# GpSimd out of the weight splits of the expert stage, layer-norm factors spread by TensorE, and a ninth gather buffer

## The chip, the cores and the metric

One core of a Trainium2 chip runs the whole program; the other cores idle. The metric is the device time of one execution in microseconds (us). The engines are TensorE (PE; its weight loads are listed as PEld), VectorE (DVE), ScalarE (ACT), GpSimd (POOL) and SyncE (SP). SyncE issues the transfers of weights and outputs, GpSimd issues the gathers, and 16 DMA engines carry out both kinds.

## The reference, cut to what matters

Two blocks follow each other on 256 tokens of width 1024, in float32. The first (a Hyena mixer and a grouped-query attention) is not touched. The second has two layers, each a mixer (a gated linear recurrence, a state-space part and windowed attention) and a product-key expert layer:

```python
def second_block(x, ...):
    h = layer_norm(x, emb_ln_g, emb_ln_b)
    for l in range(DEPTH):                       # 2
        proj = h @ w_in[l]
        ...                                      # three mixers -> mix
        h = layer_norm(DN_ALPHA * h + mix, ln1_g[l], ln1_b[l])
        ffn = peer_ffn(h, peer_wq[l], peer_keys[l], peer_u[l], peer_v[l])
        h = layer_norm(DN_ALPHA * h + ffn, ln2_g[l], ln2_b[l])
    return h

def peer_ffn(x, wq, keys, u, v):                 # per chunk of 128 tokens
    ...                                          # 8 heads x 16 experts: idx, gate
    ue = u[idx]; ve = v[idx]
    act = gelu(einsum('td,thkd->thk', xc, ue))
    return einsum('thk,thkd->td', gate * act, ve)
```

Each token picks 128 of 16384 experts (8 heads, 16 each), and each expert is one row of `u` and one of `v`, 1024 numbers each. `layer_norm` is `(x - mean) * rsqrt(var + eps) * g + b`, with `g` and `b` of 1024 numbers; there are five such pairs.

## The kernel before, in words

The second block works on four units: layer 0 and tokens 0 to 127, layer 0 and tokens 128 to 255, then the same for layer 1. Here a unit's mixer is called work 0 to 3. Work 0 runs by itself. After that the experts of unit n run together with work n + 1.

**Experts** (`experts`). For each unit 128 gathers run (512 in all). One gather fetches for each of the 128 tokens one expert's row of `u` and `v`, 8 KB per partition, 1 MB in all, into a buffer `uv`; it is an indirect DMA that GpSimd issues (line 1258). VectorE forms the dot product with the token (line 1267, "the dot"). ScalarE applies the gelu for two gathers at a time (line 1271), multiplies by the gate (line 1278) and makes a diagonal matrix `dg` (line 1281). TensorE adds `dg @ v` to two accumulating banks `psG`, two matmuls of 128x512 (line 120, "the add"). The add frees the buffer. Eight buffers exist (`UV_BUFS`), the gathers are issued four ahead of the dots (`UV_BUFS - 4`), and the add comes three gathers after the dot.

**Mixer work** (`work`, a `Flow` of generators). After each gather's instructions the loop takes some steps of the next unit's flow, so many that it ends shortly before the unit's 128 gathers do (`per`, `owed`). Its matrices (60 loads of up to 512 KB, 120 pieces) come through four raw buffers on SyncE's queue. ScalarE rounds each piece to a high part `wh` (line 77); the low part `wl` is the difference of both (line 78, "the split"). `k.share` says who makes it: with 2 every second piece's split goes to GpSimd, with 4 every fourth, else to VectorE. Work 0 has 2, works 1 to 3 have 4. TensorE then needs three matmuls a piece.

**Layer norms.** `stats` forms mean and variance on VectorE, the power on GpSimd (`rsqrt`, line 124), and loads `g` and `b`, spread over all 128 partitions by the DMA, into four tiles `lng` of 256 KB (line 810). `scaled` applies them in two steps for each half of the row (lines 830 and 831). There are ten norms: two ahead of work 0, one in each work, one at the end of each unit's experts. The tiles `lng` also hold the recurrence's gate weights `rg_w` (line 1019).

**Order.** The program is written as these loops; a scheduler then orders each engine's instructions by modelled times, and moves DMAs forward to where it models their buffers free. Each engine runs its list in order: an instruction that waits holds up all behind it on its engine. This holds for DMA issues on SyncE and GpSimd as well.

PSUM has in this stage two banks each for `G` (the adds), `M` (the main stream: projections, output, the turns), `C` and `D`.

Of the kernel before, what the change touches and what calls it, by code (L numbers as in the profile page):

```python
# [20 lines left out]
P = 128  # L21
# [619 lines left out]
def peer_route(k, pool, kb, qT, t, h0, nh, idx, gate):  # L641
# [10 lines left out]
    for h in range(nh):  # L652
        ps = k.bank("D")
        k.mm(ps[:, :SEQ], qT[:, h0 + h, t * P:(t + 1) * P], kb)
        sc = T([P, 2, P], "psc", bufs=2)
        nc.scalar.copy(sc.rearrange("p a b -> p (a b)"), ps[:, :SEQ])
        for i in range(2):
            top16(k, pool, sc[:, i, :], ts_[:, h, i, :], tu[:, h, i, :], P)
            yield
# [39 lines left out]
def top16(k, pool, vals, top, idx, n):  # L699
    nc = k.nc  # L700
    rest = pool.tile([P, P], F32, tag="trs", name=k.uid("trs"), bufs=2)[:, :n]
    nc.vector.max(top[:, 0:8], vals)
    nc.vector.max_index(idx[:, 0:8], top[:, 0:8], vals)
    nc.vector.match_replace(rest, top[:, 0:8], vals, -3.0e38)
    nc.vector.max(top[:, 8:16], rest)
    nc.vector.max_index(idx[:, 8:16], top[:, 8:16], rest)
# [31 lines left out]
UV_BUFS = 8  # L738
# [3 lines left out]
class Second:  # L742


    def __init__(self, k, io, pool, h):
        self.k, self.io, self.pool, self.h = k, io, pool, h
        self.lay, self.kb, self.qT = {}, {}, {}
        self.idx = {}
        self.po = {}
        self.rs = {}  # L750

# [51 lines left out]
    def stats(self, t, i, src):  # L803

        k, nc = self.k, self.k.nc
        gb = []
        for j in range(2):
            for dh in range(2):
                w = self.T([P, 512], "lng", bufs=4)
                nc.sync.dma_start(w, self.io["ln_gb"][i, j, dh * 512:(dh + 1) * 512].partition_broadcast(P))  # L810
                gb.append(w)
# [10 lines left out]
        self.rs[t] = gb, mv, rs  # L822

    def scaled(self, t):
        nc = self.k.nc
        gb, mv, rs = self.rs.pop(t)
        r = self.h[t]
        for dh in range(2):
            cs = slice(dh * 512, (dh + 1) * 512)
            nc.vector.scalar_tensor_tensor(r[:, cs], r[:, cs], mv[:, 0:1], gb[dh], ALU.subtract, ALU.mult)  # L830
            nc.vector.scalar_tensor_tensor(r[:, cs], r[:, cs], rs, gb[2 + dh], ALU.mult, ALU.add)  # L831
# [174 lines left out]
    def left(self, l, t):  # L1006
# [10 lines left out]
        for i in range(2):  # L1017
            wbd.append(T([P, 512], "lng", bufs=4).rearrange("p (a c) -> p a c", a=4))
# [227 lines left out]
    def experts(self):  # L1246
# [51 lines left out]
        k.share = 4  # L1298
# [157 lines left out]
def layouts(x, c, ctx, c_ctx, norm_g, ada_w, ada_b, hy_w_in, hy_conv_w, hy_conv_b, hy_fw1, hy_fb1,  # L1456
# [98 lines left out]
    io["ln_gb"] = np.stack(gb).reshape(5, 2, D)  # L1555
# [34 lines left out]
```

## Time and profile before

| | |
|---|---|
| time, median of 3 runs | 2750.16 us (2749.62 to 2754.34) |
| profiled execution | 2752.02 us, its span 2750.3 us |
| mean granted TensorE clock | 0.958 of 2.4 GHz |
| busy: TensorE, VectorE, ScalarE, GpSimd | 2364.6, 2075.2, 1294.2, 1055.5 us |
| moved by DMA | 778.11 MB; gathers (queue 0) 536.90 MB |
| first gather issued | 1094.0 us |
| last dot | 2732.8 us |

The first block and work 0 take the time up to 1094 us; the expert stage takes the rest. The page's chain of waits holds hardly more than the last norm, so the stage is read from stretches of time, from the waits and from the order of time. In a row of stretches each engine's busy time is followed by its count of instructions; PEclk is the granted clock, and the DMA share is the mean busy share of the 16 DMA engines.

### The profile page before, as it was taken

To read this page: it belongs to the slowest core of one execution; us is meant where nothing else is said; L and a number is where in the kernel's file an instruction comes from. 1 tells how busy PE (TensorE), PEld (TensorE's weight loads), DVE (VectorE), ACT (ScalarE), POOL (GpSimd) and SP (SyncE) were. 2 spreads that over 40 slices of the span, in tenths; PEclk is the share of its full clock that TensorE was granted. 3 is DMA by queue.
4 is the path that set the end of the run, shared out by engine and by line. 5 is a ranking of instruction groups with operands and counts; after the bars stand their busy time and mean duration, and the time that the engine had idled before them with its cause. 6 is when DMAs were issued, how large, how long until landed. Compare 5 with 4: busy or idle time off the path is not lost. (4 is left out here: it accounts for less than half of the span.)

```text
span 2750.3 us, 30013 instructions
## 1 busy us (share of the span) xinstructions
PE 2364.6 (86%) x8930; PEld 1463.6 (53%) x8930; DVE 2075.2 (75%) x4579; ACT 1294.2 (47%) x2960; POOL 1055.5 (38%) x844
## 2 busy tenths in 40 slices
PE   8999999999998786788978888987788998777776
PEld 4788888857888454445533344544344544322222
DVE  6788887766887876799758589867689966964444
ACT  4444444434554664467534366734366753322222
POOL 0322223221210443544445455544444454343332
PEclk9999999999999797899999999999999999899999
DMA  6333332224333554999899999999999999899997
GB/s 245 123 106 112 111 108 90 79 90 149 118 104 116 189 178 156 413 393 358 340 398 392 413 401 373 399 386 383 389 405 381 360 372 368 343 404 421 421 422 306
DMA packets 149162, 778.11 MB, mean 283 GB/s; under 512 B 18663, under 2 KB 19464, under 8 KB 83464
## 3 DMA queue, kind: packets, MB, share of 16 engines
q0 software_dynamic: 73728, 536.90, 48.2%
q1 hardware_dynamic: 75272, 239.29, 24.4%
q8 instruction: 72, 1.18, 0.2%
q14 instruction: 90, 0.74, 0.1%
HBM read 775.08 MB, written 1.05 MB: 282 GB/s over the span
## 5 line engine op out<-in xcount | busy, mean ns | idle before, releaser
L120 PE MATMUL psG<-uv,dg 128*128 128x512 f32 x2048 | 1009.5, 630 | 235.4 <-ACT dg L1281 235.0
L1267 DVE CUSTOM_DVE_ANT_0 uv<-uv,h 128x1024 f32<-128x1024 f32 x512 | 648.1, 1270 | 308.5 <-DMA uv<-in_peer_uv_dram,idx 303.9
L1258 POOL DMA_INDIRECT uv<-in_peer_uv_dram,idx x512 | 602.9, 1177 | 455.6 <-PE psG L120 266.9
L120 PEld LDWEIGHTS psG<-uv,dg 128*128 128x128 f32 x2048 | 387.9, 199 | 706.7 <-ACT dg L1281 349.8
L77 ACT ACTIVATE wh<-w 128x512 fp32r<-128x512 f32 (+3 forms) x644 | 454.0, 721 | 483.8 <-PE psA L116 178.7
L78 DVE TENSOR_TENSOR wl<-w,wh 128x512 fp32r<-128x512 f32 (+3 forms) x494 | 441.9, 909 | 126.5 <-ACT wh L77 123.3
L78 POOL TENSOR_TENSOR wl<-w,wh 128x512 fp32r<-128x512 f32 (+1 forms) x150 | 233.0, 1554 | 541.5 <-issue 362.9
L1271 ACT ACTIVATE cf<-act 128x2 f32<-128x2 f32 x256 | 51.7, 202 | 545.2 <-DVE act L1267 544.6
L117 PE MATMUL psA<-hT1h,wl 128*128 128x512 f32 (+1 forms) x640 | 235.7, 369 | 2.4 <-DVE wl L78 2.4
L115 PE MATMUL psA<-hT1h,wh 128*128 128x512 f32 (+1 forms) x640 | 236.9, 371 | 0.0
L116 PE MATMUL psA<-hT1l,wh 128*128 128x512 f32 (+1 forms) x640 | 235.6, 368 | 0.0
L116 PE MATMUL psM<-wl,hTh 128*128 128x512 f32 (+1 forms) x352 | 180.5, 513 | 42.2 <-DVE wl L78 37.0
L115 PE MATMUL psM<-wh,hTh 128*128 128x512 f32 (+1 forms) x352 | 169.6, 484 | 22.9 <-DVE idx L689 12.8
L1281 ACT ACTIVATE dg<-ident,cf 128x128 f32<-128x128 f32 x512 | 174.9, 386 | 1.0 <-PE psG L120 1.0
L117 PE MATMUL psM<-wh,hTl 128*128 128x512 f32 (+1 forms) x352 | 142.6, 405 | 0.0
L115 PEld LDWEIGHTS psA<-hT1h,wh 128*128 128x128 f32 x640 | 120.6, 188 | 23.4 <-issue 0.9
L117 PEld LDWEIGHTS psA<-hT1h,wl 128*128 128x128 f32 x640 | 120.5, 188 | 23.1 <-DVE wl L78 2.8
L116 PEld LDWEIGHTS psA<-hT1l,wh 128*128 128x128 f32 x640 | 120.6, 188 | 19.9
L116 PEld LDWEIGHTS psM<-wl,hTh 128*128 128x128 f32 x352 | 71.3, 203 | 106.7 <-DVE wl L78 60.1
L1278 ACT ACTIVATE cf<-cf,gate 128x1 f32<-128x1 f32 x512 | 122.3, 286 | 6.6
L369 POOL TENSOR_TENSOR hm<-hx,hx 128x512 f32<-128x512 f32 x16 | 30.5, 1905 | 187.5 <-ACT hx L359 187.5
L115 PEld LDWEIGHTS psM<-wh,hTh 128*128 128x128 f32 x352 | 70.8, 202 | 57.1 <-issue 23.3
(417 smaller groups left out, 3813.9 us busy)
## 6 DMA issues: line engine op xcount, KB each, us to landing
w<-in_w_in_r_dram SPq DMA_DIRECT2D x128, 512.0 KB, 7.9
w<-in_hy_w_in_dram SPq DMA_DIRECT2D x64, 512.0 KB, 3.5
w<-in_w_out_dram SPq DMA_DIRECT2D x64, 512.0 KB, 6.0
w<-in_ada_w_dram SPq DMA_DIRECT2D x32, 512.0 KB, 3.5
w<-in_peer_wq_dram SPq DMA_DIRECT2D x32, 512.0 KB, 7.8
lng<-in_ln_gb_dram SPq DMA_DIRECT2D x40, 256.0 KB, 5.6
aw<-in_ada_w_dram SPq DMA_DIRECT2D x16, 512.0 KB, 8.6
w<-in_hy_w_out_dram SPq DMA_DIRECT2D x16, 512.0 KB, 3.5
```

The costliest lines, as they stand in the source:

```text
L77: nc.scalar.activation(dst.hi, src, AF.Copy)
L78: (eng or nc.vector).tensor_tensor(dst.lo, src, dst.hi.bitcast(F32), ALU.subtract)
L115: mm(out, a.hi, b.hi, start=start, stop=False)
L116: mm(out, a.hi, b.lo, start=False, stop=False)
L117: mm(out, a.lo, b.hi, start=False, stop=stop)
L120: self.nc.tensor.matmul(out, a, b, start=start, stop=stop)
L369: nc.gpsimd.tensor_tensor(m[:, ci, :], got[0], got[3], ALU.mult)
L1258: nc.gpsimd.indirect_dma_start(out=uv.rearrange("p a b -> p (a b)"), out_offset=None, in_=self.io[f"peer_uv{n // 2}"], in_offset=bass.Indi ...
L1267: nc.vector.tensor_tensor_reduce(u, u, self.h[i // P % 2], 1.0, 0.0, ALU.mult, ALU.add, acts[i // 2][:, i % 2:i % 2 + 1])
L1271: nc.scalar.activation(cfs[b], acts.pop(b), AF.Gelu)
L1278: nc.scalar.activation(cf[:, j:j + 1], cf[:, j:j + 1], AF.Copy, scale=gate[:, c:c + 1])
L1281: nc.scalar.activation(dg, k.ident, AF.Copy, scale=cf[:, j:j + 1])
```

## The change

Three things are changed together. `k.share` is 0 in the expert stage, so VectorE makes every split of works 1 to 3; work 0 keeps 2. The factors of all norms are loaded once, as one tile of 20 rows and 512 columns (row 4i + 2j + half), and `scaled` spreads a row over the partitions with a matmul whose weights are a column of the identity repeated 128 times; VectorE then reads the factors from the two `M` banks. The space of the `lng` tiles, of one score tile `psc` and of one tile `trs` goes to a ninth gather buffer, so gathers are issued five ahead; the gate weights `rg_w` move into the work tiles `la3` and `la4`.

```diff
--- before.py
+++ after.py
@@ -652,7 +652,7 @@
     for h in range(nh):
         ps = k.bank("D")
         k.mm(ps[:, :SEQ], qT[:, h0 + h, t * P:(t + 1) * P], kb)
-        sc = T([P, 2, P], "psc", bufs=2)
+        sc = T([P, 2, P], "psc")
         nc.scalar.copy(sc.rearrange("p a b -> p (a b)"), ps[:, :SEQ])
         for i in range(2):
             top16(k, pool, sc[:, i, :], ts_[:, h, i, :], tu[:, h, i, :], P)
@@ -698,7 +698,7 @@
 
 def top16(k, pool, vals, top, idx, n):
     nc = k.nc
-    rest = pool.tile([P, P], F32, tag="trs", name=k.uid("trs"), bufs=2)[:, :n]
+    rest = pool.tile([P, P], F32, tag="trs", name=k.uid("trs"))[:, :n]
     nc.vector.max(top[:, 0:8], vals)
     nc.vector.max_index(idx[:, 0:8], top[:, 0:8], vals)
     nc.vector.match_replace(rest, top[:, 0:8], vals, -3.0e38)
@@ -735,7 +735,7 @@
 
 MIX_ORDER = [0, 1, 2, 3, 12, 13, 14, 15, 4, 5, 6, 7, 8, 9, 10, 11]
 MT_BUFS = 3
-UV_BUFS = 8
+UV_BUFS = 9
 RAWS = 4
 
 
@@ -748,6 +748,8 @@
         self.idx = {}
         self.po = {}
         self.rs = {}
+        self.gb = self.T([20, 512], "lng")
+        k.nc.sync.dma_start(self.gb, io["ln_gb"])
 
     def T(self, shape, tag, dt=F32, bufs=1):
         return self.pool.tile(shape, dt, tag=tag, name=self.k.uid(tag), bufs=bufs)
@@ -803,12 +805,6 @@
     def stats(self, t, i, src):
 
         k, nc = self.k, self.k.nc
-        gb = []
-        for j in range(2):
-            for dh in range(2):
-                w = self.T([P, 512], "lng", bufs=4)
-                nc.sync.dma_start(w, self.io["ln_gb"][i, j, dh * 512:(dh + 1) * 512].partition_broadcast(P))
-                gb.append(w)
         r = self.h[t]
         st, mv, ve, rs = self.T([P, 2, 6], "lst"), self.T([P, 2], "lmv", bufs=2), self.T([P, 1], "lve"), self.T([P, 1], "lrs", bufs=2)
         for dh in range(2):
@@ -819,16 +815,20 @@
         nc.vector.bn_aggr(mv, st.rearrange("p a b -> p (a b)"))
         nc.vector.tensor_scalar(ve, mv[:, 1:2], LN_EPS, None, ALU.add)
         k.rsqrt(rs, ve)
-        self.rs[t] = gb, mv, rs
+        self.rs[t] = i, mv, rs
 
     def scaled(self, t):
-        nc = self.k.nc
-        gb, mv, rs = self.rs.pop(t)
+        k, nc = self.k, self.k.nc
+        i, mv, rs = self.rs.pop(t)
         r = self.h[t]
         for dh in range(2):
             cs = slice(dh * 512, (dh + 1) * 512)
-            nc.vector.scalar_tensor_tensor(r[:, cs], r[:, cs], mv[:, 0:1], gb[dh], ALU.subtract, ALU.mult)
-            nc.vector.scalar_tensor_tensor(r[:, cs], r[:, cs], rs, gb[2 + dh], ALU.mult, ALU.add)
+            gb = [k.bank("M") for _ in range(2)]
+            for j in range(2):
+                row = 4 * i + 2 * j + dh
+                k.mm(gb[j], k.ident[:20, row:row + 1].broadcast_to([20, P]), self.gb)
+            nc.vector.scalar_tensor_tensor(r[:, cs], r[:, cs], mv[:, 0:1], gb[0], ALU.subtract, ALU.mult)
+            nc.vector.scalar_tensor_tensor(r[:, cs], r[:, cs], rs, gb[1], ALU.mult, ALU.add)
 
     def turned(self, t):
 
@@ -1015,7 +1015,7 @@
         d = self.lay
         wbd = []
         for i in range(2):
-            wbd.append(T([P, 512], "lng", bufs=4).rearrange("p (a c) -> p a c", a=4))
+            wbd.append(A(3 + i))
             nc.sync.dma_start(wbd[i], self.io["rg_w"][l][:, 4 * i:4 * i + 4, :])
         yield self.wait("rx")
         xc = A(0)
@@ -1295,7 +1295,7 @@
         flow.finish()
         per = flow.steps / (P - 14.0)
         lag, ahead = 3, UV_BUFS - 4
-        k.share = 4
+        k.share = 0
         flow, owed, routes = None, 0.0, iter(())
         for i in range(NS + lag):
             n, s = i // P, i % P
@@ -1552,7 +1552,7 @@
     gb = [emb_ln_g_2, emb_ln_b_2]
     for l in range(2):
         gb += [ln1_g_2[l], ln1_b_2[l], ln2_g_2[l], ln2_b_2[l]]
-    io["ln_gb"] = np.stack(gb).reshape(5, 2, D)
+    io["ln_gb"] = np.stack(gb).reshape(20, 512)
     io["peer_wq"] = np.stack([chunks(peer_wq_2[l], 512, 4) for l in range(2)])
     kb = np.zeros((2, P, 2 * P), f32)
     for i in range(2):
```

The change moves instructions on four engines. First GpSimd, in work 3 beside the gathers of unit 2 (`uv` are gather buffers, `wl` the low parts of weight pieces), before:

```order
L1258 DMA uv_17360<-in_peer_uv_dram,idx_16287 128x2048
L1258 DMA uv_17386<-in_peer_uv_dram,idx_16287 128x2048
L1258 DMA uv_17410<-in_peer_uv_dram,idx_16287 128x2048
L78 TENSOR_TENSOR wl_17447<-w_17339,wh_17446 128x512
L1258 DMA uv_17463<-in_peer_uv_dram,idx_16287 128x2048
L1258 DMA uv_17470<-in_peer_uv_dram,idx_16287 128x2048
L1258 DMA uv_17513<-in_peer_uv_dram,idx_16287 128x2048
L78 TENSOR_TENSOR wl_17533<-w_17437,wh_17532 128x512
```

and after, where the same gathers have numbers that are 4 higher:

```order
L1258 DMA uv_17364<-in_peer_uv_dram,idx_16291 128x2048
L1258 DMA uv_17390<-in_peer_uv_dram,idx_16291 128x2048
L1258 DMA uv_17414<-in_peer_uv_dram,idx_16291 128x2048
L1258 DMA uv_17467<-in_peer_uv_dram,idx_16291 128x2048
L1258 DMA uv_17474<-in_peer_uv_dram,idx_16291 128x2048
L1258 DMA uv_17517<-in_peer_uv_dram,idx_16291 128x2048
```

The gathers now follow each other; of 90 splits in the three works none is left on GpSimd.

VectorE at the same place (piece pairs of the raw tile `w_17339`; the other names belong to the routing and to a convolution), before:

```order
L685 TENSOR_TENSOR poh_17424<-poh_17424,pti_16900 128x512
L78 TENSOR_TENSOR wl_17440<-w_17339,wh_17439 128x512
L686 TENSOR_REDUCE pix_4445_17422<-poh_17424 128x32
L1002 SCALAR_TENSOR_TENSOR sd_4455_17453<-xp_17433,bcw_13167,sd_4455_17453 128x128 x4
L1267 ISA uv_17329,act_17412<-uv_17329,h_8063 128x1024
L1267 ISA act_17412 128x1
L1002 SCALAR_TENSOR_TENSOR sd_4455_17453<-xp_17433,bcw_13167,sd_4455_17453 128x128
L1267 ISA uv_17360,act_17472<-uv_17360,h_8063 128x1024
```

and after, where that raw tile is `w_17343`:

```order
L78 TENSOR_TENSOR wl_17444<-w_17343,wh_17443 128x512
L679 TENSOR_TENSOR pbf_17378<-ppf_17376,pa_4435_17380 128x32
L685 TENSOR_TENSOR poh_17428<-poh_17428,pti_16904 128x512
L78 TENSOR_TENSOR wl_17451<-w_17343,wh_17450 128x512
L686 TENSOR_REDUCE pix_4447_17426<-poh_17428 128x32
L1002 SCALAR_TENSOR_TENSOR sd_4457_17457<-xp_17437,bcw_13171,sd_4457_17457 128x128 x6
L1267 ISA uv_17289,act_17416<-uv_17289,h_8063 128x1024
L1267 ISA act_17416 128x1
L1267 ISA uv_17333,act_17476<-uv_17333,h_8063 128x1024
```

Both halves of the raw tile are now split on VectorE, and here the mixer's instructions stand one dot earlier among the dots (`uv_17289` had been passed by then before). In work 1 they stand some seven dots earlier, in works 2 and 3 within a few of where they were.

TensorE at the first two norms (`h_8063` is the first token tile, `psA` the end of the first block, `psM` the `M` banks), before:

```order
L1440 MATMUL psA_8034<-ident,x 128x128 x4
L840 MATMUL psM_8176<-ident,h_8063 128x128 x4
L840 MATMUL psM_8183<-ident,h_8063 128x128 x4
L115 MATMUL psM_8190<-wh_8191,hTh_8174 128x272
L116 MATMUL psM_8190<-wl_8192,hTh_8174 128x272
```

and after:

```order
L1440 MATMUL psA_8034<-ident,x 128x128 x4
L120 MATMUL psM_8084<-lng_8073,ident 128x512
L120 MATMUL psM_8085<-lng_8073,ident 128x512
L120 MATMUL psM_8090<-lng_8073,ident 128x512
L120 MATMUL psM_8091<-lng_8073,ident 128x512
L120 MATMUL psM_8105<-lng_8073,ident 128x512
L120 MATMUL psM_8106<-lng_8073,ident 128x512
L120 MATMUL psM_8111<-lng_8073,ident 128x512
L120 MATMUL psM_8112<-lng_8073,ident 128x512
L840 MATMUL psM_8178<-ident,h_8063 128x128 x4
L840 MATMUL psM_8185<-ident,h_8063 128x128 x4
L115 MATMUL psM_8192<-wh_8193,hTh_8176 128x272
```

The matmuls that spread the factors of both token tiles stand ahead of the turn of the first (line 840), with which work 0 begins. On SyncE the forty `lng` loads are replaced by one of 40 KB.

## Rows read from the trace of the kernel before

**Rows 1.** The page: the span, and the DMA engines in forty slices, tenths.
```profile
span 2750.3 us, 30013 instructions
DMA  6333332224333554999899999999999999899997
```
**Rows 2.** Two stretches: busy time of each engine, clock, DMA share, GB/s.
```profile
1094.00:2440.00 1346.00, 1127.50 (x3486) 592.25 (x3487) 1081.06 (x2811) 703.04 (x1814) 658.92 (x502) 0.94 0.96 382
2440.00:2720.00 280.00, 207.79 (x448) 80.61 (x446) 138.34 (x226) 70.55 (x279) 106.61 (x112) 1.00 1.01 421
```
**Rows 3.** Stretches of 100 us: PE, PEld, DVE, ACT, POOL, clock, DMA share, GB/s.
```profile
1200.00:1300.00 100.00, 86.17 (x320) 50.05 (x319) 95.08 (x279) 65.29 (x157) 44.63 (x36) 0.95 0.91 360
1300.00:1400.00 100.00, 92.39 (x328) 51.26 (x327) 75.50 (x170) 54.50 (x135) 49.49 (x38) 0.95 0.91 365
...
1600.00:1700.00 100.00, 85.79 (x276) 48.31 (x275) 94.39 (x233) 69.33 (x172) 55.90 (x38) 0.97 0.95 375
...
2000.00:2100.00 100.00, 86.63 (x277) 48.21 (x277) 89.62 (x216) 64.52 (x167) 53.77 (x38) 0.97 1.00 398
2100.00:2200.00 100.00, 88.80 (x354) 51.88 (x352) 92.55 (x244) 75.96 (x165) 47.04 (x36) 0.97 0.92 364
```
**Rows 4.** Waits of POOL, 1094 to 2440 us: us in total, times, longest.
```profile
POOL wl L78 <- issue: 359.7, 77, 12.8
POOL uv L1258 <- PE psG L120: 133.4, 87, 9.2
...
POOL wl L78 <- ACT wh L77: 30.7, 6, 7.5
```
**Rows 5.** POOL in order of time: start, us, idle before and what ended it.
```profile
1281.42 1.43 POOL L1258 DMA_INDIRECT uv<-in_peer_uv_dram,idx  x1 [0.55 <-PE psG L120]
1293.17 1.28 POOL L78 TENSOR_TENSOR wl<-w,wh 128x512 fp32r<-128x512 f32 x1 [10.33 <-issue]
1294.60 1.24 POOL L1258 DMA_INDIRECT uv<-in_peer_uv_dram,idx  x1
1296.14 1.60 POOL L1258 DMA_INDIRECT uv<-in_peer_uv_dram,idx  x1 [0.30 <-issue]
```
**Rows 6.** Groups, 1094 to 2440 us: count, busy us, mean ns, idle before.
```profile
L1267 DVE CUSTOM_DVE_ANT_0 uv<-uv,h 128x1024 f32<-128x1024 f32 x395 | 504.8, 1284 | 161.0 <-DMA uv<-in_peer_uv_dram,idx 158.0 <-PE psG L120 1.8 <-ACT hTh L77 0.7
L78 DVE TENSOR_TENSOR wl<-w,wh 128x512 fp32r<-128x512 f32 (+1 forms) x268 | 177.4, 685 | 35.8 <-ACT wh L77 35.5
L702 DVE MAX8 pts<-psc 128x8 f32<-128x128 f32 x57 | 15.5, 282 | 5.6 <-ACT psc L656 5.6
L1258 POOL DMA_INDIRECT uv<-in_peer_uv_dram,idx x400 | 496.1, 1240 | 281.0 <-PE psG L120 133.4 <-issue 55.6 <-DVE ptu L706 21.0
L78 POOL TENSOR_TENSOR wl<-w,wh 128x512 fp32r<-128x512 f32 (+1 forms) x90 | 152.3, 1692 | 390.5 <-issue 359.7 <-ACT wh L77 30.7
```
**Rows 7.** Groups, 2500 to 2700 us, where only gathers run.
```profile
L1267 DVE CUSTOM_DVE_ANT_0 uv<-uv,h 128x1024 f32<-128x1024 f32 x80 | 98.0, 1225 | 100.8 <-DMA uv<-in_peer_uv_dram,idx 100.8
L1258 POOL DMA_INDIRECT uv<-in_peer_uv_dram,idx x81 | 77.2, 953 | 123.9 <-PE psG L120 92.1 <-DVE act L1267 29.2 <-issue 2.6
```
**Rows 8.** Tile `lng` on SP, 1094 to 2740 us: ns min/median/max.
```profile
L810 SPq DMA_DIRECT2D lng<-in_ln_gb_dram x26: 327/328/1180, 1169.9 to 2428.5; - x26
```
**Rows 9.** Tile `psG` (ns min/median/max), and a wait of PE, 1094 to 2440 us.
```profile
L120 PE MATMUL psG<-uv,dg x2048: 590/592/1222, 1106.3 to 2738.2; 128*128 128x512 f32 x187
...
PE psG L120 <- ACT dg L1281: 158.8, 91, 9.8
```
**Rows 10.** Order of time at the first norms.
```profile
892.78 0.75 DVE L830 SCALAR_TENSOR_TENSOR h<-h,lmv,lng 128x512 f32<-128x512 f32 x1 [1.53 <-DMA lng<-in_ln_gb_dram]
...
895.32 1.94 PE L840 MATMUL psM<-ident,h 128*128 128x128 f32 x8 [7.92 <-DVE h L831]
```
**Rows 11.** Order of time at the end.
```profile
2741.04 1.40 DVE L830 SCALAR_TENSOR_TENSOR h<-h,lmv,lng 128x512 f32<-128x512 f32 x2
...
2742.36 1.41 DVE L831 SCALAR_TENSOR_TENSOR h<-h,lrs,lng 128x512 f32<-128x512 f32 x2
```

## The prediction

> **What bounds the kernel now.** I read the forty slices of the page first, then the stretches, the waits of the engines that stand between two gathers, the order of time on GpSimd, and last the groups of instructions and the two ends of the stage.
>
> The slices split the run in two. For the first sixteen of them the DMA engines are at two to six tenths; after that, from about 1100 us, they are at eight or nine. The change touches this second stage, where 512 gathers of 1.05 MB (128 rows of 8 KB) feed the experts, and the ten layer norms ahead of and inside it. The span is 2750.3 us [rows 1]; the profiled execution took 2752.0 us, 1.9 us over the median of 2750.16; the sum is made against 2752.0 and those 1.9 us come off at the end.
>
> In the stage there are two kinds of stretch. From 2440 us on there is nothing but gathers: the DMA engines are full and move 421 GB/s, while every compute engine has time to spare. That stretch has a floor, 1.05 MB / 421 GB/s = 2.49 us a gather, and no part of the change moves it. From 1094 to 2440 us the mixer work of the next token tile runs beside the gathers. There the share of the DMA engines is 0.96 and the rate 382 GB/s, with TensorE at 1127 of 1346 us, VectorE at 1081 and GpSimd at 659 [rows 2]. So 0.04 x 1346 = 54 us of DMA time go unused there. They lie where the mixer is thickest: the share is 0.91, 0.91, 0.95 and 0.92 in four of the stretches of 100 us, and three of these have VectorE at 92 to 95 [rows 3].
>
> Why do the engines run dry, when four gathers are meant to be ahead? GpSimd works in order, and one of four weight splits stands in its queue between the gathers. It waits 360 us in 77 places for such a split's input, and 31 us more in 6 others, against 133 us for a buffer that TensorE must release [rows 4]. The order of time shows what that does: after the gather at 1281.4 GpSimd stands for 10.3 us before a split, runs it in 1.3 us, and then issues the next two gathers with 0.3 us or less before each: their buffers had been free behind the split [rows 5]. Waits and runs together, 390 + 152 us over 90 splits, are 6.0 us per split in which no gather is issued, more than two gathers' worth of DMA time.
>
> **The change part by part.**
>
> *GpSimd splits no more weights in the stage.* 90 splits leave GpSimd (1.692 us each) and go to VectorE, where the same operation takes 0.685 us [rows 6]: +62 us. VectorE gets something back. A dot takes 1.284 us in the mixer stretches and 1.225 us among gathers alone, where GpSimd splits nothing [rows 6, 7]: 395 x 0.059 = 23 us. Other VectorE operations under a split should shorten too, which no row separates, so the net is 0 to +39 us on 1081. I take +39, or 2.9 us in 100. A rule of the Trainium skill speaks against this part (SBUF — State Buffer, section "SBUF: two separate sides"): a VectorE operation with two SBUF inputs and a GpSimd operation that reads SBUF take a shared port in turn, each for its whole length, and descriptors are written through it. By that rule each moved split can now hold up a gather, 62 us at most if all 90 did, and the longer gather instruction of the mixer stretches (1.240 us, against 0.953 us among gathers alone, rows 6 and 7) fits it. That time would go onto a queue that loses 542 us of splits and their waits, so the sum is the same by the rule and without it.
>
> *What of the 54 us comes back.* In the three stretches with VectorE at 95, 94 and 92 the DMA engines idle for 9 + 5 + 8 = 22 us; VectorE has 5 + 6 + 7 us left there, less 2.9 each for its own growth, so I count 9. Of the other 32 us I count 28, since the gather then waits for its buffer alone, and the ninth buffer lets it be issued one add earlier. That is -37 us, between 0 and -54. One rule of the Trainium skill (DMA: Bandwidth & Descriptors, section "Where 436 GB/s comes from") would give none of it: it puts the limit between HBM and SBUF at about 358 GB/s for a core. The trace does not agree: 382 GB/s already in the mixer stretches and 421 GB/s for 280 us on end [rows 2]; by the rule the sum would be that of the rival "only the bytes".
>
> *Norm factors.* In the stage 26 transfers of 256 KB go [rows 8], 6.8 MB; at 421 GB/s that is -16 us where the DMA engines are the limit, and nothing where they are not. In their place come four matmuls per norm from one small tile. The nearest row is the fp32 128x512 matmul of the adds: 2048 instructions for 1024 calls, so two an output, at 0.592 us [rows 9]; that is 4.7 us a norm, and 6 norms in the mixer stretches make 28 us of TensorE time. TensorE waits 159 us for scaled diagonals in the same stretches [rows 9], which hides nearly all of it. What it does not hide is the order: only two banks exist for the spread factors, so the third matmul waits for VectorE's first step and the fourth for its second, which waits for GpSimd's power; the adds queued behind stand meanwhile, and then gathers wait for their buffers. Three to four gathers in flight cover some 8 to 10 us of that. Between 0 (not below: TensorE did none of this before) and +28; I take +3, near the covered end.
>
> *The first two norms, ahead of the stage.* VectorE no longer waits for the factors (1.5 us at 892.8), but now all eight spreading matmuls of both token tiles stand ahead of the first turn of the stream in TensorE's order. Before, the turn starts at 895.3, right after the third norm step [rows 10]; after, it must wait for the second tile's norm too, which goes through the two banks in turn: four pairs of a VectorE step (0.75) and a matmul (about 1.2). I estimate a start near 900, +5 us. The weight loads that stood behind eight factor transfers come sooner, so part of it may be made good: -3 to +10, I take +5. Work 0's own second norm gains two waits of about a matmul: +2 us.
>
> *The end.* Today both first steps, then both second steps follow each other at 2741.0 to 2743.8 [rows 11]. After, the last step needs a matmul that starts when the bank of the third is read: +1 us. Its cover would be TensorE's idleness, and there is none, since the bank is what is late.
>
> *Costed at nothing.* The order of VectorE's list puts the mixer of work 1 some seven dots earlier, and that of works 2 and 3 about where it was; the same work stands in the same 128 gathers, so I count no time for it. One score tile instead of two: ScalarE's next copy waits for VectorE's search, five operations of about 0.28 us [rows 6], or 1.4 us. ScalarE, at 703 of 1346 us [rows 2], has 640 us to hide it in; without that cover 32 copies make 45 us. The rest tile is written and read by VectorE alone, in order. The gate weights now go into two work tiles of the layer, so on SyncE their loads wait for the last readers in the tile before, and the weight loads queued behind them wait too. Three loads are held ahead for that; if they ran out, six waits of a few us each would show.
>
> Sum: 2752.0 - 37 - 16 + 3 + 5 + 2 + 1 = 2710; less 1.9 against the median, 2708 us.
>
> **Rivals.**
> *All of the idle time comes back.* VectorE does not grow, because everything under a split gets shorter: 2752 - 54 - 16 + 8 - 2 = 2688. For it speaks that the burst after each split shows free buffers; against it VectorE at 95.
>
> *Only the bytes.* With splits gone, the gathers wait for TensorE's adds as long as they waited behind the splits, since dots and adds set the pace: 2752 - 16 + 11 - 2 = 2745. For it speaks that 133 us are already waits for a buffer [rows 4]; against it that the waits before splits are 390 us. That the moved work does not do what is said (gathers go out no earlier) ends here too.
>
> *VectorE sets the pace.* The place is the mixer stretches with VectorE at 89 or more (four, rows 3). They hold at least 4/13.5 of 90 splits, 27, and up to 40 as the mixer is thicker there: 40 x 0.685 = 27 us straight onto the end, nothing of the idle DMA time back, the bytes worthless because transfers are no longer late, and the 11 us of the norms on top: 2752 + 27 + 11 - 2 = 2788. It decides from the point where VectorE exceeds 97 in those stretches while dots no longer wait for gathers. Against it: VectorE is at 80 percent over the mixer stretches as a whole.
>
> **How the numbers follow.** Forecast, 2695 to 2730: 0.52. All idle time back, under 2695: 0.24. Only the bytes, 2735 to 2755: 0.16. VectorE sets the pace: 0.08. A measurement of this kernel tells a change from none at about 0.2%, 5.5 us. The first two cases and half of the third are faster: 0.84; the other half is the same: 0.08; slower 0.08. The range leaves out the slow case and the lower end of the second: 2675 to 2750.
>
> **What would show it.** In the profile after: GpSimd has no split from 1094 us on and waits before gathers for TensorE alone; the DMA share of the mixer stretches is 0.98 or more and the last stretch still moves 421 GB/s; VectorE's dots there come down to about 1.23 us while its busy share rises by 0 to 3 in 100; the turn of the first tile starts near 900 us. Wrong would be the step on idle time if the share stayed at 0.96 with VectorE over 97 in the thick stretches, the one on bytes if the stage shortened by less than its share rose, and the one on norms if TensorE showed waits of 5 us and more before the fourth spreading matmul, with dry DMA engines behind them.

## The result, and the profile after

The kernel after takes 2683.5 us (median of six runs, 2676.2 to 2690.7) against 2748.7 us for the kernel before on the same chip: a ratio of 0.9768, 95% interval 0.9745 to 0.9790. It is faster by 65 us, where 42 were forecast; the range, 2675 to 2750, holds the time. The profiled execution took 2687.9 us, so its own 4 us over the median are in every row below.

Its page, the two lines that answer to [rows 1]:

```profile
span 2686.1 us, 30160 instructions
...
DMA  6333332223332344799999999999999999899997
```

The first gather is issued at 1105.9 us (1094.0 before) and the last dot starts at 2668.9 (2732.8 before). So the start of the stage came 11.9 us later, the stage itself became 75.7 us shorter (1563.0 for 1638.7), and what follows it is as long as before: 64 us of span in all.

The whole stage of after in one row, in the columns of [rows 2] (PE, PEld, DVE, ACT, POOL, clock, DMA share, GB/s), and under it its mixer part, its pure-gather part, and the stretches of 100 us that answer to [rows 3]:

```profile
1105.90:2668.90 1563.00, 1346.81 (x3987) 676.06 (x3988) 1213.05 (x3130) 775.61 (x2102) 598.91 (x524) 0.96 0.99 402
...
1106.00:2370.00 1264.00, 1121.45 (x3498) 588.03 (x3499) 1067.03 (x2890) 700.44 (x1807) 487.21 (x408) 0.95 0.98 399
2370.00:2650.00 280.00, 211.72 (x460) 82.47 (x458) 137.09 (x223) 70.10 (x276) 109.77 (x114) 1.00 1.01 420
...
1200.00:1300.00 100.00, 92.87 (x350) 53.24 (x350) 99.02 (x290) 70.65 (x167) 41.65 (x30) 1.00 1.02 415
1300.00:1400.00 100.00, 94.82 (x333) 50.20 (x333) 82.02 (x188) 56.49 (x145) 39.18 (x33) 0.98 1.01 410
1600.00:1700.00 100.00, 89.97 (x286) 49.81 (x285) 96.04 (x263) 66.16 (x164) 35.50 (x30) 0.95 1.00 404
...
2000.00:2100.00 100.00, 85.71 (x280) 47.41 (x281) 91.27 (x243) 70.63 (x171) 33.18 (x28) 0.97 0.97 394
2100.00:2200.00 100.00, 96.58 (x394) 55.38 (x393) 90.53 (x235) 69.95 (x170) 37.44 (x32) 0.98 0.96 389
```

Beside the mixers the rate is 399 GB/s for 382, and in the thick stretch at 1200 us the DMA engines are full while VectorE is busy 99 of 100. The pure-gather part is what it was (420 GB/s). One number matters most, VectorE's busy time over the stage. The same row of before, from its first gather to its last dot:

```profile
1094.00:2732.80 1638.80, 1345.34 (x3955) 676.98 (x3956) 1225.61 (x3047) 776.57 (x2104) 765.71 (x614) 0.95 0.97 388
```

1225.6 us there, 1213.1 after: VectorE took on 90 more splits and is busy 12.6 us less.

The waits of GpSimd from 1106 to 2370 us, and the groups there, against [rows 4] and [rows 6]:

```profile
POOL uv L1258 <- PE psG L120: 405.8, 194, 10.1
POOL uv L1258 <- DVE wl L78: 55.2, 19, 6.5
```

```profile
L1258 POOL DMA_INDIRECT uv<-in_peer_uv_dram,idx x396 | 477.6, 1206 | 762.3 <-PE psG L120 405.8 <-DVE wl L78 55.2 <-DVE act L1267 47.5
L1267 DVE CUSTOM_DVE_ANT_0 uv<-uv,h 128x1024 f32<-128x1024 f32 x393 | 475.2, 1216 | 54.4 <-DMA uv<-in_peer_uv_dram,idx 49.0 <-ACT dg L1281 2.8 <-PE psG L120 2.5
L78 DVE TENSOR_TENSOR wl<-w,wh 128x512 fp32r<-128x512 f32 (+1 forms) x354 | 233.6, 671 | 59.1 <-ACT wh L77 57.5 <-issue 0.3
```

GpSimd now waits mostly for a buffer that TensorE's add must free (405.8 of 762.3 us before gathers); a dot takes 1.216 us beside the mixers, no more than the 1.225 among gathers alone [rows 7]; and the dots' waits for gathers fell from 158 to 49 us.

The norms, on tile `lng` of TensorE (ns min/median/max, and who waited for it: us, times), then the order of time on TensorE at the first norms, against [rows 8, 10]:

```profile
L120 PE MATMUL psM<-lng,ident x80: 587/691/1217, 892.5 to 2680.8; 20*128 20x512 f32 x80
...
  DVE h L830: 20.4, 11
```

```profile
892.46 13.99 PE L120 MATMUL psM<-lng,ident 20*128 20x512 f32 x16 [3.79 <-DMA lng<-in_ln_gb_dram]
906.38 2.03 PE L840 MATMUL psM<-ident,h 128*128 128x128 f32 x8
```

The sixteen spreading matmuls of the two first norms, in turn with VectorE's steps through two banks, hold TensorE from 892.5 to 906.4 us; over all norms VectorE's first step waits 20.4 us for such a matmul; the first tile's turn came at 895.3 before. Two of VectorE's steps in a row show the length of one turn, 1.7 us:

```profile
897.96 0.75 DVE L830 SCALAR_TENSOR_TENSOR h<-h,lmv,psM 128x512 f32<-128x512 f32 x1 [0.70 <-PE psM L120]
...
899.66 0.75 DVE L831 SCALAR_TENSOR_TENSOR h<-h,lrs,psM 128x512 f32<-128x512 f32 x1 [0.68 <-PE psM L120]
```

### The profile page after: what moved, and what is told of

It reads as the page before. It is cut to its first block, busy times and chain, and to the rows that moved or that the text cites. A ratio compares the mean times of both kernels' runs of the same rounds, so it can differ in the third digit from the quotient of the medians.

```text
span 2686.1 us, 30160 instructions
## 1 busy us (share of the span) xinstructions
PE 2396.8 (89%) x9010; PEld 1475.2 (55%) x9010; DVE 2066.8 (77%) x4669; ACT 1295.3 (48%) x2963; POOL 888.4 (33%) x754
## 4 chain that ended last, share of the span: by engine, by line
PE 51%; DVE 18%; DMA 15%; issue 7%; ACT 5%; POOL 4%; SPq 0%; POOLq 0%; DVEq 0%; ACTq 0%
PE psG L120 13%; DMA uv<-in_peer_uv_dram,idx 11%; PE psA L115 7%; PE psA L117 7%; PE psA L116 7%; DVE uv L1267 6%; DVE wl L78 2%; POOL wl L78 2%; PE psM L116 2%; PE psA L120 2%; PE psM L117 2%; PE psM L115 2%; DMA w<-in_w_in_r_dram 2%; POOL uv L1258 1%; PE psM L120 1%
## 5 line engine op out<-in xcount | busy, mean ns | idle before, releaser
L120 PE MATMUL psG<-uv,dg 128*128 128x512 f32 x2048 | 984.7, 622 | 161.3 <-ACT dg L1281 161.1
L1258 POOL DMA_INDIRECT uv<-in_peer_uv_dram,idx x512 | 589.2, 1151 | 935.4 <-PE psG L120 539.2
L1267 DVE CUSTOM_DVE_ANT_0 uv<-uv,h 128x1024 f32<-128x1024 f32 x512 | 621.1, 1219 | 208.0 <-DMA uv<-in_peer_uv_dram,idx 201.1
L78 DVE TENSOR_TENSOR wl<-w,wh 128x512 fp32r<-128x512 f32 (+2 forms) x584 | 501.3, 867 | 149.2 <-ACT wh L77 144.7
L116 PE MATMUL psM<-wl,hTh 128*128 128x512 f32 (+1 forms) x352 | 164.7, 468 | 43.6 <-DVE wl L78 38.2
L1281 ACT ACTIVATE dg<-ident,cf 128x128 f32<-128x128 f32 x512 | 175.7, 387 | 14.8 <-PE psG L120 14.7
L78 POOL TENSOR_TENSOR wl<-w,wh 128x512 fp32r<-128x512 f32 (+1 forms) x60 | 81.7, 1363 | 161.6 <-ACT wh L77 159.9
```

The source lines that it names most:

```text
L78: (eng or nc.vector).tensor_tensor(dst.lo, src, dst.hi.bitcast(F32), ALU.subtract)
L116: mm(out, a.hi, b.lo, start=False, stop=False)
L120: self.nc.tensor.matmul(out, a, b, start=start, stop=stop)
L1258: nc.gpsimd.indirect_dma_start(out=uv.rearrange("p a b -> p (a b)"), out_offset=None, in_=self.io[f"peer_uv{n // 2}"], in_offset=bass.Indi ...
L1267: nc.vector.tensor_tensor_reduce(u, u, self.h[i // P % 2], 1.0, 0.0, ALU.mult, ALU.add, acts[i // 2][:, i % 2:i % 2 + 1])
L1281: nc.scalar.activation(dg, k.ident, AF.Copy, scale=cf[:, j:j + 1])
```

## The experiments

All runs in one table. The difference to after is that of the ratios, times 2749 us. "Stage" is from the first gather's issue to the last dot's start. "Free to issue" is the mean time from the end of the add that frees a gather buffer to the issue of the gather into it (gathers 10 to 383), worked out from the starts and ends of the instructions in each trace. By the intervals a difference to after is known to about 10 us (13 for e5), so the 10 us of e3 and of e8 and the 15 of e5 are only just clear of nothing.

| run | ratio to before (95%) | us | to after, us | first gather | stage | VectorE busy in it | free to issue |
|---|---|---|---|---|---|---|---|
| before | 1 | 2748.7 | +64 | 1094.0 | 1638.7 | 1225.6 | 3.95 |
| after | 0.9768 (0.9745–0.9790) | 2683.5 | 0 | 1105.9 | 1563.0 | 1213.1 | 0.44 |
| e1_share_only | 0.9747 (0.9718–0.9775) | 2681.3 | −6 | 1095.3 | 1568.5 | 1214.9 | 0.39 |
| e2_norms_only | 1.0019 (1.0002–1.0036) | 2756.2 | +69 | 1104.8 | 1640.3 | 1221.3 | 3.91 |
| e3_eight_bufs | 0.9804 (0.9776–0.9832) | 2695.8 | +10 | 1110.1 | 1567.5 | 1213.1 | 0.39 |
| e4_splits_back | 0.9916 (0.9886–0.9945) | 2728.2 | +41 | 1106.1 | 1609.4 | 1224.9 | 5.87 |
| e5_wait | 0.9821 (0.9778–0.9863) | 2698.5 | +15 | 1105.7 | 1576.2 | 1216.0 | 1.43 |
| e6_port | 1.0001 (0.9983–1.0018) | 2748.1 | +64 | 1103.1 | 1625.4 | 1276.5 | 0.57 |
| e7_first_by_dma | 0.9752 (0.9712–0.9791) | 2675.4 | −4 | 1095.8 | 1556.4 | 1213.6 | 0.46 |
| e8_dve | 0.9803 (0.9780–0.9826) | 2692.1 | +10 | 1105.1 | 1568.9 | 1272.1 | 0.46 |
| e9_busy | 0.9755 (0.9732–0.9779) | 2678.7 | −4 | 1103.6 | 1557.5 | 1215.1 | 0.53 |
| e10_both_waits | 0.9837 (0.9809–0.9864) | 2702.1 | +19 | 1106.5 | 1577.8 | 1217.7 | 3.70 |
| e11_dve_dense | 0.9896 (0.9867–0.9925) | 2716.4 | +35 | 1106.6 | 1583.5 | 1261.0 | 0.44 |
| e12_one_dma | 0.9764 (0.9741–0.9787) | 2677.8 | −1 | 1095.6 | 1563.2 | 1213.9 | 0.42 |

**Which part carries the gain (e1 to e4).** The first theory was the prediction's: gathers stand behind waiting splits in GpSimd's queue (A). Its rivals gave the gain to the ninth buffer (B) or to the bytes of the factors (C).

e1, the kernel before with one line changed:

```
-        k.share = 4
+        k.share = 0
```

> The kernel before with one line changed: no split on GpSimd in the expert stage; factors by DMA and eight buffers stay. Theory A (the gathers were held up in GpSimd's in-order list behind splits whose input was not there): most of the gain of 65 us is this line, 2695 to 2712 us, DMA share of the mixer stretches 0.98 or more. Rival B (the ninth buffer carries it): 2730 or more. Rival C (the bytes of the factors carry it): 2725 or more.

e2, the kernel after with the splits on GpSimd again and eight buffers, so that only the norms (and the smaller tiles) are left of the change:

```
-UV_BUFS = 9
+UV_BUFS = 8
...
-        k.share = 0
+        k.share = 4
```

> The changed kernel with every fourth split back on GpSimd and eight buffers, so that only the spread factors (and the smaller tiles) differ from before. A: the stage gains some 20 us of DMA time at most and the part ahead of the stage loses 12, 2735 to 2750 us. C: 2700 to 2720 us.

e3, after with `UV_BUFS = 8` alone:

> The changed kernel with eight gather buffers, gathers four ahead. A: the ninth buffer only smooths, 2684 to 2696 us. B: 2710 us or more.

e4, after with `k.share = 4` alone, nine buffers:

> The changed kernel with every fourth split back on GpSimd; spread factors and nine buffers stay. A: the gathers stand behind the splits again, 2720 to 2740 us, GpSimd waits some 350 us before splits. B: the ninth buffer covers the waits, 2685 to 2700 us.

The one line of e1 gives all of the gain, and somewhat more than A had said. The norms alone (with the smaller tiles) cost 5 us (e2, interval 0.5 to 10) and with the splits gone 16 (e3 against e1), most of them ahead of the stage: the first gather comes 10.7 and 14.8 us later, and the stage is as long with the factors by TensorE (1567.5) as by DMA (1568.5). From the first norm's statistics to the first tile's turn it is 7.2 and 7.4 us in before and e1, and 16.7 to 17.2 in each of the ten runs that spread the first factors by TensorE: some 9.6 us more. What the first gather moves beyond that differs from run to run in the first block and in work 0. The ninth buffer is worth 10 us without the splits (after against e3) and 28 with them (e4 against e2). C fell; B is a part.

**What the splits cost: their waits or their work (e5, e6).** e5 gives GpSimd back a wait without the work: one column of each fourth piece.

```
+                if self.idx and not k.share and k.nw % 4 == 0:
+                    o = self.T([P, 1], "dum", bufs=2)
+                    nc.gpsimd.tensor_tensor(o, raw[:, 0:1], s.hi[:, 0:1].bitcast(F32), ALU.subtract)
```

> The kernel after, with one tiny GpSimd instruction (128x1) behind every fourth weight piece in the stage: it reads one column of the raw weight piece and one of its high half, so it waits for ScalarE's copy as the removed split did, but it works for well under 1 us and does not hold up ScalarE's or TensorE's work. Theory A (the gathers stood behind a waiting instruction in GpSimd's in-order queue): most of the gain of share 0 with nine buffers goes, 2705 to 2740 (near the 2728 of the run that put the splits back), and GpSimd's waits name ScalarE and the weight pieces again. Theory P (the split's own work on GpSimd, 1.7 us x 90, slowed VectorE or kept GpSimd busy): the time stays at 2678 to 2695.

e6 gives it back the work without the wait, beside the gathers (`old` is an activation two pairs back):

```
+                if n < 3 and s % 4 == 2 and 4 < s < 124:
+                    o, m = T([P, 2, P], "dum"), k.msk[:, 0:2, :]
+                    old = held[i // 2 - 2][:, 0:1].unsqueeze(2).broadcast_to([P, 2, P])
+                    for _ in range(2):
+                        nc.gpsimd.tensor_tensor(o, m, old, ALU.mult)
```

> The kernel after, with two GpSimd multiplications of 128x256 at 90 places of the stage, of constants and of an old column, which have nothing to wait for: about as much GpSimd work as the 90 splits (some 150 us), without their waits; their result is not used. Theory A (waits in the queue): 2680 to 2700. Theory P (GpSimd's work itself, beside VectorE): the mean dot goes from 1219 ns back toward 1270 and the time to 2710 to 2735.

e5, at 2698 us, lies between what A (2705 or more) and what P (2695 or less) had said: the wait alone costs 15 us. e6 missed both by more: GpSimd work that waits for nothing costs 64 us, the whole gain, while the gathers still leave 0.57 us after their buffer is free. The groups of GpSimd in e5 and in e6, from the first gather to 2440 us (count, busy us, mean ns, idle before):

```profile
L793 POOL TENSOR_TENSOR dum<-w,wh 128x1 f32<-128x1 f32 x88 | 49.3, 560 | 268.6 <-ACT wh L77 59.3 <-DVE act L1270 46.7 <-issue 33.6
```

```profile
L1316 POOL TENSOR_TENSOR dum<-msk,act 128x256 f32<-128x256 f32 x180 | 140.0, 778 | 3.6
```

268.6 us of waiting in the queue against 3.6: GpSimd's work alone, without waiting, hurt more than the waiting alone.

**Time on GpSimd, time on VectorE, or data (e8, e9).** e8 is e6 with `nc.vector` in place of `nc.gpsimd`; e9 has three one-column GpSimd operations at the same places:

```
+                    o, m = T([P, 1], "dum"), k.msk[:, 0, 0:1]
+                    for _ in range(3):
+                        nc.gpsimd.tensor_tensor(o, m, held[i // 2 - 2][:, 0:1], ALU.mult)
```

> The kernel after, with two VectorE multiplications of 128x256 at the same 90 places of the stage where the run with GpSimd's extra work had two GpSimd ones: some 60 us of VectorE work more, as much as VectorE's busy time had grown there (1213 to 1277 us in the stage), and nothing on GpSimd; the results are not used. Theory V (GpSimd's work costs time because it lengthens VectorE's own instructions, and VectorE sets the pace in the stretches beside the mixers): 2725 to 2755, as in that run (2748). Theory O (GpSimd's work costs time because the gathers are issued late behind it): VectorE's 60 us partly hide under the waits for gathers, 2684 to 2712.

> The kernel after, with three tiny GpSimd instructions (128x1, about 0.56 us each by the run with the waits) at the same 90 places: GpSimd is kept from its gathers about as long as by the splits (some 150 us in all), with no waits and hardly any data moved. Theory V: VectorE's busy time stays at 1213 us in the stage and the time at 2680 to 2692. Theory O: 2710 to 2750, VectorE's busy time unchanged.

Keeping GpSimd from the gathers by 116 us of tiny operations costs nothing (e9): O fell, though e8 alone would have fitted it. VectorE work spread over the works costs 10 us of 59 (e8): V as it was put fell too. What is left is what only e6 does: GpSimd moving data while VectorE works. Line 1267 (the dots) of e6 and then of e9, ns min/median/max:

```profile
L1267 DVE CUSTOM_DVE_ANT_0 uv<-uv,h x512: 1161/1219/2030, 1109.1 to 2728.5; 128x1024 f32<-128x1024 f32 x171
```

```profile
L1267 DVE CUSTOM_DVE_ANT_0 uv<-uv,h x512: 1160/1218/1312, 1109.3 to 2661.1; 128x1024 f32<-128x1024 f32 x171
```

The median dot is the same; the longest is 2030 against 1312 ns. In e4 one can watch it happen. First VectorE, then GpSimd, in order of time (start us, us):

```profile
1175.46 0.60 DVE L1002 SCALAR_TENSOR_TENSOR la<-xp,bcw,la 128x128 f32<-128x128 f32 x2
1175.98 0.68 DVE L78 TENSOR_TENSOR wl<-w,wh 128x512 fp32r<-128x512 f32 x1
1176.59 1.44 DVE L1002 SCALAR_TENSOR_TENSOR la<-xp,bcw,la 128x128 f32<-128x128 f32 x1
...
1176.59 1.28 POOL L78 TENSOR_TENSOR wl<-w,wh 128x512 fp32r<-128x512 f32 x1 [3.11 <-issue]
```

The convolution step that took 0.30 us a moment before takes 1.44 when it starts with GpSimd's split, and ends just behind it. Over e4's mixer part I sorted VectorE's instructions by whether one of GpSimd's tensor operations ran beside any part of them: a dot takes 1.215 us alone (321) and 1.524 beside one (73); the 128x128 convolution step on line 1002 0.342 and 0.992; line 702's search, with one input, 0.274 alone (77) and 0.276 beside (9) in e6. But it is not the number of inputs that decides: in e6 the shift on line 674, with one input of 128x32, takes 0.196 us alone (9) and 0.659 beside (6), while in e4 a step with two inputs of which one is a PSUM bank (line 1205) takes 0.334 alone (15) and 0.340 beside (9). Summed over all kinds of operation in e6's mixer part, the time beside GpSimd's work above the mean alone is 62.9 us, which is practically all by which VectorE's busy time in the stage grew (1213.1 to 1276.5 us). In e9 the same sum is 0.7 us, and in e5, beside the one-column operations, a dot takes 1.218 us as it does alone.

**Both waits, and VectorE's time where it has none (e10, e11).** e10 makes TensorE wait for GpSimd's queue too, again with next to no data:

```
+                if self.idx and not k.share and k.nw % 4 == 0:
+                    nc.gpsimd.tensor_tensor(s.lo[:, 0:2], raw[:, 0:2], s.hi[:, 0:2].bitcast(F32), ALU.subtract)
```

> The kernel after, but of every fourth weight piece in the stage GpSimd writes two columns of the low half again once VectorE has made it (the same values): now the gathers stand behind an instruction that waits for the piece, as in the run with the tiny instruction alone (2698), and TensorE's use of the piece waits for GpSimd's queue too, as it did with the splits; next to no data is moved. Theory W (the splits' cost beyond those 15 us is this second wait: TensorE waits for a piece that stands behind a gather that waits for TensorE): 2715 to 2735, as with the splits put back (2728), and the time from a freed buffer to its next gather goes from 0.45 us to several us. Theory V (the rest is VectorE's instructions lengthened beside GpSimd's data work): 2690 to 2705, as with the tiny instruction alone.

e11 is e8 with four operations per place, and the places `if n < 3 and s % 4 == 2 and 16 < s < 64`:

> The kernel after, with four VectorE multiplications of 128x256 at every fourth dot from the 16th to the 64th of the first three works alone, where VectorE is busy all the time (busy 49.5 to 51 us of the 51 to 53 us that 16 dots take there): 36 places, some 60 us of VectorE work in all, as in the run that spread it over the whole works (2692), and nothing on GpSimd. Theory V (the 64 us of the run with GpSimd's extra work are VectorE's, paid where VectorE has no idle time): those stretches lengthen nearly one for one, 2715 to 2745. The rival (GpSimd's data work costs time in another way, and VectorE's work is hidden by the gathers): 2685 to 2705.

e10's waits are those of the splits, as its group from the first gather to 2440 us shows:

```profile
L792 POOL TENSOR_TENSOR wl<-w,wh 128x2 fp32r<-128x2 f32 x89 | 59.4, 667 | 419.8 <-issue 195.5 <-DVE wl L78 156.9 <-DVE yms L1223 15.4
```

419.8 us before 89 of them (390.5 before the 90 splits, rows 6), and gathers 3.70 us late (3.95 in before). Yet it costs 19 us, where e4 costs 41: W fell. The other 22 us of e4 (some 11 either way) are what is left when the waits are taken off: the data that its splits move, less what VectorE saves by not making those splits itself. e11 costs 35 us for 48 us more of VectorE's busy time, where e8 costs 10 for 59. In nine groups of 16 dots (dots 16 to 64 of the first three works), where VectorE is busy 457 of after's 488 us, e8 takes 496 us, e11 515 and e6 530; VectorE is busy 475, 491 and 495 us of them. So VectorE's time is dear where it has little idle time, and there GpSimd's work lengthens it; 42 of e6's 64 us lie in these groups. The other 22 are not explained by a run: in the rest of the three works e8's 41 us of VectorE's time cost nothing, and e6's 25 us cost 19. One candidate that no run tests is the transfers themselves. The packets of the gathers' queue take 287 to 289 ns on average in the four runs in which GpSimd moves data beside the gathers (before, e2, e4, e6) and 284 to 286 in the ten others; over e6's stage that is 20 us of DMA time more than in after. It does not go with late gathers, since e10 is among the ten.

**A version that would beat both (e7, e12).** After, with the factors of the first three norms loaded into two gather buffers that no gather needs yet:

```
+        for i in range(2):
+            self.fac[i] = self.T([P, 2, D], "uv", bufs=UV_BUFS)
+            for j in range(4):
+                k.nc.sync.dma_start(self.fac[i][:, j // 2, j % 2 * 512:(j % 2 + 1) * 512], io["ln_gb"][4 * i + j].partition_broadcast(P))
...
+            if i == 0 or i == 1 and t == 0:
+                gb = [self.fac[i][:, j, cs] for j in range(2)]
```

> The kernel after, but the first two norms and that of the first work take their factors from two gather buffers that are filled by broadcast DMAs long before, when no gather needs them; the norms of the stage stay on TensorE's spreading. If the 11 to 12 us ahead of the stage are the price of spreading in the first norms: the turn is at 894 to 897 us, the first gather at 1093 to 1097, and the time 2668 to 2676, below both kernels and below the run with share 0 alone (2681). If that part is paid elsewhere (the first gathers or the loads of weights set the start): the time stays at 2680 to 2690.

e12 fills each of the two buffers by one DMA:

> The run whose first norms take their factors by DMA (2675), with one broadcast DMA per norm in place of four, so that the factors land some 2 us earlier (the eight loads were issued from 891.0 to 894.4 us and the first norm waited 1.5 us for them): 2669 to 2678, turn at 896 to 899. It is to settle with five rounds whether such a kernel beats the kernel after (2683.5, ratio 0.9768) and the run with share 0 alone (2681, ratio 0.9747): a ratio of 0.972 to 0.9745 if the 8 to 11 us ahead of the stage are kept, 0.975 or more if not.

The place was right: the first gather is back at 1095.8 and 1095.6 us, and both medians, 2675.4 and 2677.8, lie below after's. But the ratios, 0.9752 and 0.9764, lie within the intervals of after (0.9768) and of e1 (0.9747). That either beats after or the one-line change is not shown.

## Why the prediction was right, and where it was not

*The bound.* Right in part: the thick stretches, which had idle DMA time, gave the gain. Their share went from 0.91, 0.91 and 0.95 to 1.02, 1.01 and 1.00; those from 2000 and 2100 us stayed below that (1.00 to 0.97 and 0.92 to 0.96). Yet idle DMA time is only half of it. The times of all packets in the stage, over 16 engines, come to 1585.3 us before and 1544.3 after, so of the 75.7 us that the stage lost, 35 were idle DMA time and 41 were packet time (roughly: shares of 1.02 show that packets overlap a little). The reading of the waits held: the rows call most of them "issue", but 82 of the 83 splits that waited in before start within 0.15 us of the end of a high part on ScalarE.

*VectorE grows by 39 us.* This is the step that failed. The working let only the dots recover (23 us) and took the upper end of "0 to +39" for the rest, since no row separated the other operations under a split. VectorE's busy time fell by 12.6 us in the stage: 90 splits of 0.68 us came to 62 us, and everything else became 74 us shorter, of which the dots are 27 (648.1 to 621.1 us over all 512). A row for it could have been read before: in the trace of before too, the convolution step takes 1.064 us beside a split and 0.343 alone, and summed over all operations the time beside splits above the mean alone is some 60 us. VectorE's share of the mixer stretches still rose by 4 in 100 (80 to 84), more than the 0 to 3 forecast, because the stretches became shorter.

*−37 us of idle time.* Too small. The runs take the stage apart: the splits alone make it 70.2 us shorter (e1), bytes and norms together 1.0 (e3), the ninth buffer 4.5 (after). Of the 70.2 us, 45 are idle DMA time and 25 are packet time with the same bytes. The first goes with the step on VectorE, which left 13 us idle in the stretches where VectorE was said to have no room. The second had no term in the sum, and no run shows its cause. The time is near the rival "All of the idle time comes back", 2688 us, and the runs bear out its reason, that all under a split gets shorter; that its number fits is partly luck, since its 54 us of idle time and 16 of bytes stand against 35 and 41 measured, and its sum leaves out the +3 for the norms in the stage. As to the cause the prediction named one, the waits in GpSimd's queue, and the runs show two: the waits are worth 15 to 19 us (e5, e10), and 22 more of the 41 that the splits cost with nine buffers go with the data they move.

*The rule on the shared port.* The prediction weighed the Trainium skill's page "SBUF — State Buffer", section "SBUF: two separate sides" (a GpSimd operation and a VectorE operation in a two-port mode, or one with two SBUF inputs where the GpSimd operation reads SBUF, exclude each other, and the one that starts first has the ports for its whole length), and said that the sum is the same with it and without. It looked only at VectorE holding up the gather; the rule also says that GpSimd holds up VectorE, and e4's rows agree: 1.44 us for a step of 0.30, over a split of 1.28. That direction was the missing term. The direction that it did weigh does not show: with 90 more splits on VectorE the gather instruction beside the mixers takes 1.206 us, 1.240 before. e9 and e5 add that GpSimd operations of one column do not lengthen VectorE's (a dot 1.218 us beside and alone in e5).

*−16 us for the bytes, +3 for the norms in the stage.* Together −13 forecast, −1 measured (1567.5 against 1568.5 us, e3 and e1). The trace says more than the times: the packets take 13 us less in e3 (1547.2 for 1560.6), and the DMA engines idle 12 us more (20.3 for 8.0); between e2 and before it is 16 less and 17.5 more. So the bytes saved about the transfer time that was forecast, and it came back as idle time. Whether the spreading matmuls cost it, or the stage would not have been shorter by it anyway, no run separates.

*+5 us for the first norms.* Too small: the turn came 11.1 us later (906.4 for 895.3), of which 1.3 us lie ahead of the norms (the statistics start at 889.4 for 888.1) and 9.8 in them, at the upper end of −3 to +10. The prediction counted four turns through the two banks, those of the second tile, at 0.75 + 1.2 us. Eight outputs pass in turn, those of the first tile too, at 1.7 us each, and where 1.5 us of waiting for the factors was to go, TensorE first waited 3.8 us for the small tile.

*+2 us for work 0's own norm.* From the turn to the first gather it is 199.6 us for 198.7 before, but the runs with the same norms differ by more than that among themselves (197.3 to 202.0).

*+1 us at the end.* The last norm step now ends 8.4 us after the first one starts to add (2674.2 to 2682.6), 5.8 before: +2.6. The rows that answer to [rows 11]:

```profile
2680.18 0.75 DVE L830 SCALAR_TENSOR_TENSOR h<-h,lmv,psM 128x512 f32<-128x512 f32 x1 [1.30 <-PE psM L120]
2681.89 0.75 DVE L831 SCALAR_TENSOR_TENSOR h<-h,lrs,psM 128x512 f32<-128x512 f32 x1 [0.96 <-PE psM L120]
```

From the last dot's start to the end of the span it is 17.2 us for 17.5, so nothing of it is left.

*The ninth buffer* was folded into the −37; it is worth 10 us here, and would be worth 28 beside the splits. *Costed at nothing*: no run tests the smaller tiles by themselves; in e3 they are part of the −1 us above.

## What to carry to other kernels

Before moving work between GpSimd and VectorE, sort VectorE's instructions by whether GpSimd moves data beside them: count for a GpSimd operation not only its own time but what it adds to the VectorE operations under it; here 90 operations of 1.7 us on the idler engine cost more than 90 of 0.7 us on the busier one. A long wait in the queue that issues prefetches looks like the culprit, but put the wait back by itself before believing it: 420 us of it cost 19. Compare DMA time by its two parts, idle time and the time of the packets: here only half of the gain was idle time. And a broadcast that hides in a transfer queue is not made cheaper by TensorE when it stands at the head of a stage, where nothing hides the turns through two banks.

## What the runs showed of the hardware that was not expected

- A GpSimd operation of one column took 0.20 to 1.65 us, median 0.32, in e9, and the 270 of them lengthened VectorE's operations by 0.7 us in all; one of 128x256 took 0.62 us at least, and 180 of them lengthened VectorE's operations by 62.9 us (e6).
- The DMA engines moved the same gathers in the same time with the factors on top: 406 GB/s over the stage in e1 (636 MB) and 401 in e3 (628 MB), 1568.5 and 1567.5 us long.
- 60 us more of VectorE's work, spread over the stage, cost 10 us (e8) although VectorE was already at 91 to 99 of 100 in several stretches: 18 of them, in the nine groups above, cost 8 us, and the 41 in the rest of the three works cost nothing.
- Gather packets took 287 to 289 ns on average in the runs in which GpSimd moved data beside the gathers and 284 to 286 in the others; why, no run shows.
